# Decoder layer: the down projection's buffers laid out anew, and the work behind the last unit of the up projection put in another order

## The chip, the cores and the metric

The kernel runs on one core of one Trainium2 chip. The metric is the device time of one execution in microseconds (us). A profiled execution is the source of all views shown here; times inside it count from the start of its span.

## The reference

One decoder layer on 1024 tokens with 1024 channels, float32. Three branches (an mLSTM, a differential attention, a cross-attention into 256 memory tokens) are merged by gates and projected; then comes the MLP, which is the part this change touches:

```python
D_MODEL = 1024
SEQ = 1024
D_FF = 4 * D_MODEL
...
        x = x + merged @ w_out[l]

        h2 = rms_norm(x, norm_mlp_g[l])
        x = x + jnp.square(jax.nn.relu(h2 @ w_up[l])) @ w_down[l]
```

## The kernel before, in words

Float32 products are made from three passes of TensorE: every operand is split into a rounded part and the rest (`split`, lines 106 to 117: ScalarE casts, VectorE subtracts), and `mm3` (line 88) issues three matmuls, first*first, first*rest, rest*first. Nearly all matmuls of the kernel stand therefore under line 93.

The MLP is computed with seven products in place of eight for each 2x2 block of tiles (Winograd's form of Strassen's scheme). `PROD` lists the seven pairs: which of seven sums of weights meets which of seven sums of activations. A *step* is one such block: 7 products x 3 = 21 matmuls of 128x512.

Up projection, `wino`: 16 *units*. Each has four steps (one for each pair of input blocks `kp`), and its seven products gather in seven of PSUM's eight banks `p0` to `p6`; the next unit takes the banks shifted by one. After a unit VectorE combines the seven banks into four tiles (`c11`, `u2`, `u3`, `c21`), and `use_up` multiplies them by the normalisation `rb`, ScalarE takes relu and square into `rq`, and `wino_t` makes four sums `xts` of the squares (lines 1242 to 1245: t0 = b0-b1, t2 = b2-b0 on GpSimd always, t1 = b2-t0, t3 = b3-t1). The three plain tiles (`r_d<-rq`, issued by ScalarE) and the four sums (`r_d<-xts`, issued by SyncE) are stored to the DRAM buffer `r_d`, one entry for each unit: 7 planes of 128x512. Unit u is operand q = u of the down projection.

Down projection, `down`: 16 passes of four steps, `passes = [(p % 4, range(p, 4 + p))]`. Pass p works for output group p % 4 with operands q = p to p + 3. An operand is fetched back from `r_d` in two or three parts into `xd` tiles (`xdma`: three planes and four, or 3 + 2 + 2), and each part is split in place (`xsplit`: ScalarE cast, VectorE subtract). Operand 0 lies in pools x00 (planes 0 to 2), x01 (3, 4) and x02 (5, 6); operands 1, 2, 3 in x1, x2, x3; later ones take these places over in turn. This text calls the two parts of operands 1 to 3 "1a" (three planes) and "1b" (four planes) and so on; 4a, 4b, 4c are the three parts of operand 4.

Weights, `wino_steps`: `raw()` loads 256 KB of raw weights (`wraw`, SyncE) and has GpSimd make four sums of 128x128 (lines 1260 to 1263); `wsp(n)` splits the seven sums into a weight pair `wo` (ScalarE cast, VectorE subtract, 128x896 each) and issues the next `raw()`. `wrp` and `wop` are rings of places for raw weights and pairs, `lead` says how many steps ahead of its use a pair is made. `side(n)`, called behind step n, makes the next pair, fetches the operand whose place has come free, and splits parts of the one that is needed two or three steps later.

The sums over passes lie in SBUF accumulators `acc`. Behind the first pass of each group four of them are loaded with the residual (`acc<-x_d`, 256 KB each, SyncE), VectorE subtracts one from another, and then adds the banks to them; the next pass may overwrite a bank only when that has been done.

What sets the order: TensorE and all VectorE work that goes through `self.V` (class `InOrder`) stand in the order of the program text while `self.pinned` is set. Everything on `nc.scalar`, `nc.gpsimd`, `nc.sync` and plain `nc.vector` (so also `self.split`, in contrast to `self.split2`) is placed in its engine's queue by the scheduler of the build. Each engine then runs its queue strictly in order. SyncE's queue holds nearly all loads and stores: a store that waits for its data holds back all loads behind it. Pools are laid into SBUF one behind the other, so which place of `down` lies on which place of `wino` decides when the first loads of `down` may start.

Of the kernel before, what the change touches and what calls it, by code (L numbers as in the profile page):

```python
# [73 lines left out]
class Layer:  # L74
# [1340 lines left out]
    def tail(self):  # L1415
        tc, nc, a = self.tc, self.nc, self.a
        V, G = nc.vector, nc.gpsimd
# [9 lines left out]
        with ExitStack() as c0:  # L1427
# [4 lines left out]
            rb = one.tile([P, D], F32, name="rb2")  # L1432
# [63 lines left out]
            with ExitStack() as c1:  # L1496
                E = lambda *x, **k: c1.enter_context(tc.tile_pool(*x, **k))
                one_ = lambda n: E(name=n, bufs=1)
# [17 lines left out]
                def use_up(u, cs):  # L1516

                    b = self.xrp.tile([P, 4, 512], F32, tag="xr", name=self.name("rq"))
                    V_, M = (nc.vector, G) if u == 15 else (self.V, self.V)
                    for i in (1, 3, 2, 0):  # L1520
                        hf = i % 2
                        M.tensor_mul(cs[i], cs[i], rb[:, hf * 512 : (hf + 1) * 512])
                        self.A.activation(cs[i], cs[i], AF.Relu)
                        self.A.activation(b[:, i], cs[i], AF.Square)
                    self.A.dma_start(self.rd[u, :, 0:3], b[:, 1:4])
                    yield
                    t = self.wino_t(b, V_)
                    nc.sync.dma_start(self.rd[u, :, 3:7], t)
                    yield

# [34 lines left out]
    def down(self):  # L1565
# [4 lines left out]
        with ExitStack() as c1:  # L1570
            one_ = lambda n: c1.enter_context(tc.tile_pool(name=n, bufs=1))

            def accum(pool, n, pad):
                accs.extend(pool.tile([P, 512], F32, name=f"acc{len(accs) + i}") for i in range(n))
                if pad:
                    pool.tile([P, pad], F32, name=self.name("pad"))
# [8 lines left out]
            wr = [one_("dwr0"), one_("dwr1")]  # L1585
            a2 = one_("acc2")
            accum(a2, 4, 0)
            wr.append(one_("dwr2"))
            a3 = one_("acc3")
            accum(a3, 8, 768)  # L1590
            x1, x2 = one_("dx1"), one_("dx2")
            x02, wr = one_("dx02"), Ring(wr)
            wo = Ring([one_(f"dwo{i}") for i in range(3)])
            x00 = one_("dx00")
            accs = accs[2:] + accs[:2]
            xp = (((x00, 0, 3), (x01, 3, 2), (x02, 5, 2)), *(((x, 0, 3), (x, 3, 4)) for x in (x1, x2, x3)))
            acc = [accs[7 * g : 7 * g + 7] for g in range(4)]
# [5 lines left out]
            passes = [(p % 4, tuple(range(p, 4 + p))) for p in range(16)]  # L1603
            last = len(passes) - 1
            steps = [(g, q) for g, qs in passes for q in qs]
            raw, wsp, W = self.wino_steps([a["wdown"][g][:, kp(q)] for g, q in steps], wr, wo, 2)
            X, use1, use9 = {}, {}, {}
            for n, (g, q) in enumerate(steps):
                use1.setdefault(q, n)
# [2 lines left out]
            def xdma(q):  # L1612

                X[q] = []
                for pool, i, n in xp[q % 4]:
                    t = pool.tile([P, n, 2, 512], F32R, tag=f"x{i}", name=self.name("xd"))
                    nc.sync.dma_start(f32(t[:, :, 1]), self.rd[kp(q), :, i : i + n])
                    X[q].append(t)
# [22 lines left out]
                        xsplit(q, (1, 2))  # L1641

            xdma(0)
            raw()
            raw()
            xsplit(0, split=self.split)
            wsp(0, self.split, False)
            xdma(1)
            xsplit(1, split=self.split)
            wsp(0)  # L1650
            xdma(2)
            xsplit(2, (0,))
            wsp(0)
            xsplit(2, (1, 2))
            xdma(3)
            n = -1
            seen = set()
            for p, (g, qs) in enumerate(passes):
# [7 lines left out]
                for run in (qs[0:1], qs[1:2], qs[2:4]) if p == last else [(q,) for q in qs]:  # L1666
                    for j, (l, x) in enumerate(self.PROD):
                        for i, q in enumerate(run):
                            w = W[n + 1 + i]
                            self.mm3(ps[j], (w[:, l, 0], w[:, l, 1]), operand(q, x), q == qs[0], q == qs[-1])  # L1670
                    n += len(run)
                    if q != qs[-1]:
                        side(n)
                if new:

# [230 lines left out]
```

## Time and profile before

| what | value |
|---|---|
| median of three runs | 2195.51 us (2194.28 to 2201.09) |
| the profiled execution's own time | 2196.3 us |
| its span (first to last instruction) | 2194.5 us |
| TensorE (PE) matmul busy | 2150.9 us, 98% of the span |
| VectorE (DVE) busy | 1418.6 us, 65% |
| ScalarE (ACT) busy | 1002.7 us, 46% |
| GpSimd (POOL) busy | 565.5 us, 26% |
| mean granted TensorE clock | 0.996 |
| up projection, matmuls out of `xo` | 1344, 307.0 us busy |
| down projection, matmuls out of `xd` | 1344, 310.5 us busy, the first at 1871.98 us |

The profile's rows read "start us, us, engine, line, operation, out<-in, how many in a row, and in brackets the idle time before with what ended it". Buffer numbers are left out there: `wo` is any weight pair, `xd` any part of an operand, `p` any PSUM bank. SPq is SyncE's queue. The table says that TensorE sets the time; what can be won or lost by a change at the joint of the two projections is idle time of TensorE there, and the matmuls that it then runs at a lower clock.

### The profile page before, as it was taken

Reading aid. Unit: us, or ns where it says so; the run is one execution under the profiler, and the core shown is the slowest. Engines: PE = TensorE matmul, PEld = TensorE weight load, DVE = VectorE, ACT = ScalarE, POOL = GpSimd, SP = SyncE. Lnnn points to the kernel's source line nnn. Section 1 sums busy time; section 2 is a strip of 40 time slices with the busy share of each in tenths; the row PEclk is TensorE's granted clock in tenths of the full one; section 3 lists DMA queues with packets and bytes.
Section 4 is the critical chain, followed back from the end, with each engine's and each line's share of the span. In section 5 each row is a group of like instructions: output and inputs, shape, how many; then the busy total and the mean of one; then the engine's idle time right before and its main releaser. Section 6 shows DMA issues by size and latency. Waiting matters only on the chain.

```text
span 2194.5 us, 30706 instructions
## 1 busy us (share of the span) xinstructions
PE 2150.9 (98%) x11049; PEld 1852.4 (84%) x11049; DVE 1418.6 (65%) x2674; ACT 1002.7 (46%) x1998; POOL 565.5 (26%) x736
## 2 busy tenths in 40 slices
PE   7999999999999999999999999999999999899999
PEld 5877888898899999999888788888888788688887
DVE  6643565575548778777655433554688987767779
ACT  6543354454346666666554221223435444543332
POOL 2100000000111111111121002202756665655552
PEclk9999999999999999999999999999999999999999
DMA  6123122121443433333343643435434544844444
GB/s 246 36 73 116 59 92 68 45 81 49 161 115 92 96 97 91 84 84 83 109 148 133 207 143 127 146 111 191 154 121 173 194 155 148 328 163 158 142 142 168
DMA packets 137358, 281.46 MB, mean 128 GB/s; under 512 B 13137, under 2 KB 29814, under 8 KB 135158
## 3 DMA queue, kind: packets, MB, share of 16 engines
q1 hardware_dynamic: 130870, 259.58, 37.5%
q10 hardware_dynamic: 6336, 19.93, 2.3%
q8 instruction: 87, 1.43, 0.3%
q14 instruction: 65, 0.53, 0.1%
HBM read 182.95 MB, written 71.34 MB: 116 GB/s over the span
## 4 chain that ended last, share of the span: by engine, by line
PE 87%; DVE 5%; DMA 3%; ACT 2%; issue 1%; POOL 1%; SPq 0%; DVEq 0%; ACTq 0%; POOLq 0%
PE mm L93 51%; PE p L93 23%; PE sc L93 6%; PE po L93 3%; PE tp L96 3%; DVE acc L69 1%; DVE u L69 1%; PE pr L96 1%; DMA kraw<-y 1%; DVE wo L69 0%; DMA xd<-r_d 0%; DVE c L69 0%; PE tp L93 0%; DVE w L114 0%; DMA mx<-in_mem 0%
## 5 line engine op out<-in xcount | busy, mean ns | idle before, releaser
L93 PE MATMUL mm<-w,hT 128*128 128x384 f32 (+3 forms) x2496 | 470.6, 330 | 4.1 <-ACT w L113 3.5
L93 PE MATMUL mm<-hT,w 128*128 128x512 f32 x1680 | 413.2, 397 | 0.0
L93 PEld LDWEIGHTS mm<-w,hT 128*128 128x128 f32 x2496 | 387.7, 189 | 15.9 <-ACT w L113 4.3
L93 PEld LDWEIGHTS mm<-hT,w 128*128 128x128 f32 x1680 | 309.6, 189 | 65.1
L93 PE MATMUL p<-xd,wo 128*128 128x512 f32 x1344 | 310.5, 393 | 7.4 <-DVE xd L69 1.6
L93 PE MATMUL p<-xo,wo 128*128 128x512 f32 x1344 | 307.0, 390 | 1.2 <-DVE u L69 1.2
L93 PEld LDWEIGHTS p<-xd,wo 128*128 128x128 f32 x1344 | 253.7, 189 | 64.1 <-DVE xd L69 2.6
L93 PEld LDWEIGHTS p<-xo,wo 128*128 128x128 f32 x1344 | 251.6, 188 | 55.2 <-DVE u L69 2.8
L93 PE MATMUL mm<-kt,w 128*128 128x512 f32 x1152 | 264.1, 391 | 4.7 <-ACT kt L113 3.6
L93 PEld LDWEIGHTS mm<-kt,w 128*128 128x128 f32 x1152 | 216.9, 189 | 51.8 <-ACT kt L113 4.7
L113 ACT CAST w<-raw 128x256 fp32r<-128x256 f32 (+3 forms) x272 | 142.1, 545 | 166.6 <-PE mm L93 120.2
L106 ACT CAST wo<-wraw 128x896 fp32r<-128x896 f32 x124 | 116.8, 944 | 213.7 <-PE p L93 98.4
L114 DVE TENSOR_TENSOR w<-raw,w 128x256 fp32r<-128x256 f32 (+3 forms) x272 | 161.5, 614 | 79.9 <-ACT w L113 79.0
L69 DVE TENSOR_TENSOR wo<-wraw,wo 128x896 fp32r<-128x896 f32 x124 | 143.6, 1172 | 59.1 <-ACT wo L106 59.1
L1260 POOL TENSOR_TENSOR wraw<-wraw 128x128 f32<-128x128 f32 x128 | 93.7, 732 | 246.2 <-DMA wraw<-in_wdown 109.5
L1008 ACT ACTIVATE dpe<-sc,dst,drr 128x256 f32<-128x256 f32 (+7 forms) x128 | 106.6, 833 | 97.5 <-DVE dst L1004 95.2
L129 POOL TENSOR_SCALAR hss<-hss 128x4 f32<-128x4 f32 x8 | 3.3, 408 | 414.9 <-ACT mscr L754 273.0
L1000 DVE CUSTOM_DVE_ANT_0 sc<-sc,tmask 128x256 f32<-128x256 f32 (+7 forms) x128 | 97.0, 758 | 13.3 <-PE sc L93 12.7
L93 PE MATMUL sc<-dk,dq 128*128 128x512 f32 (+3 forms) x384 | 92.2, 348 | 0.0
L106 ACT CAST xd<-xd 128x1536 fp32r<-128x1536 f32 (+2 forms) x38 | 58.3, 1535 | 68.6 <-DMA xd<-r_d 68.6
L1263 POOL TENSOR_TENSOR wraw<-wraw 128x128 f32<-128x128 f32 x128 | 86.6, 676 | 10.0
L1262 POOL TENSOR_TENSOR wraw<-wraw 128x128 f32<-128x128 f32 x128 | 88.9, 694 | 0.0
(313 smaller groups left out, 3083.9 us busy)
## 6 DMA issues: line engine op xcount, KB each, us to landing
dk<-dsg SPq DMA_DIRECT2D x64, 256.0 KB, 4.5
wraw<-in_wup SPq DMA_DIRECT2D x64, 256.0 KB, 2.9
r_d<-xts SPq DMA_DIRECT2D x16, 1024.0 KB, 4.1
wraw<-in_wdown SPq DMA_DIRECT2D x64, 256.0 KB, 3.0
xd<-r_d SPq DMA_DIRECT2D x19, 768.0 KB, 7.3
xd<-r_d SPq DMA_DIRECT2D x14, 1024.0 KB, 6.4
raw<-in_wd SPq DMA_DIRECT2D x32, 384.0 KB, 3.3
gl<-gates SPq DMA_DIRECT2D x48, 256.0 KB, 2.7
```

Of the source, the lines that this page charges most:

```text
L69: return self.tc.keep_in_program_order(f(*a, **k))
L93: self.pin(self.nc.tensor.matmul(out, l, r, start=start, stop=stop))
L96: self.pin(self.nc.tensor.transpose(out, x, self.ident))
L106: self.A.copy(hi, src)
L113: nc.scalar.copy(hi, src)
L114: nc.vector.tensor_sub(lo, src, f32(hi))
L129: g.tensor_scalar(r, ss, 1.0 / width, EPS, op0=ALU.mult, op1=ALU.add)
L1000: V.tensor_tensor_reduce(out=sc[:, 0:n], in0=sc[:, 0:n], in1=self.tmask[:, D - n : D], scale=1.0, scalar=-3.0e38, op0=ALU.add, op1=ALU.max ...
L1008: nc.scalar.activation(pe[c][:, 0:n], sc[:, 0:n], AF.Exp, bias=t8[:, 2 + c : 3 + c], scale=rr[:, i, c : c + 1], accum_out=t8[:, 4 + c : 5 ...
L1260: G.tensor_add(r[:, 4], r[:, 0], r[:, 3])
L1262: G.tensor_sub(r[:, 6], r[:, 1], r[:, 0])
L1263: G.tensor_sub(r[:, 7], r[:, 2], r[:, 5])
```

## The change

It touches three things.

1. Places. `down` now has four places for raw weights and four for pairs (three each before), pairs are made three steps ahead (`lead` 3, before 2), and the last part of operand 0, x02, has a place at the top of SBUF. By the addresses of the build, x02 lay on two raw places of the up projection before, and lies on no place of it now; the four raw places and four pair places are now just those of the up projection.
2. The start of `down`: four raw loads first, then operands 1, 2 and 3 in one go; x02 of operand 0 is split beside x00 and x01; three pairs are made with `self.split` ahead of the first pass, and operand 2 is left to `side`.
3. Behind the last unit (u = 15): the four multiplications by `rb` go from GpSimd to VectorE, in the pinned order; three of the four sums `xts` go from VectorE to GpSimd, which then makes all four; and what `side(0)` issues on VectorE stands behind the last of the four multiplications (`tc.issue_after`).

```diff
                     b = self.xrp.tile([P, 4, 512], F32, tag="xr", name=self.name("rq"))
-                    V_, M = (nc.vector, G) if u == 15 else (self.V, self.V)
                     for i in (1, 3, 2, 0):
                         hf = i % 2
-                        M.tensor_mul(cs[i], cs[i], rb[:, hf * 512 : (hf + 1) * 512])
+                        self.after = self.V.tensor_mul(cs[i], cs[i], rb[:, hf * 512 : (hf + 1) * 512])
...
-                    t = self.wino_t(b, V_)
+                    t = self.wino_t(b, G if u == 15 else self.V)
...
-            wr.append(one_("dwr2"))
+            wo = [one_("dwo0")]
             a3 = one_("acc3")
-            accum(a3, 8, 768)
+            accum(a3, 8, 0)
             x1, x2 = one_("dx1"), one_("dx2")
-            x02, wr = one_("dx02"), Ring(wr)
-            wo = Ring([one_(f"dwo{i}") for i in range(3)])
-            x00 = one_("dx00")
+            wr = Ring(wr + [one_("dwr2"), one_("dwr3")])
+            wo = Ring(wo + [one_(f"dwo{i}") for i in (1, 2, 3)])
+            x00, x02 = one_("dx00"), one_("dx02")
...
-            raw, wsp, W = self.wino_steps([a["wdown"][g][:, kp(q)] for g, q in steps], wr, wo, 2)
+            raw, wsp, W = self.wino_steps([a["wdown"][g][:, kp(q)] for g, q in steps], wr, wo, 3)
...
             xdma(0)
-            raw()
-            raw()
+            for _ in range(4):
+                raw()
+            xdma(1)
+            xdma(2)
+            xdma(3)
+            xsplit(2)
             xsplit(0, split=self.split)
-            wsp(0, self.split, False)
-            xdma(1)
+            wsp(0, self.split)
             xsplit(1, split=self.split)
-            wsp(0)
-            xdma(2)
-            xsplit(2, (0,))
-            wsp(0)
-            xsplit(2, (1, 2))
-            xdma(3)
+            wsp(0, self.split)
+            wsp(0, self.split)
...
-                    if q != qs[-1]:
+                    if n == 0:
+                        with tc.issue_after(self.after.ins):
+                            side(n)
+                    elif q != qs[-1]:
                         side(n)
```

How the built programs differ at three places. First VectorE's queue about 150 us before the end of the up projection, where the combining of a unit meets the splits of operand 0; with `xd` the parts x01 (2 planes) and, in the changed program, x02. Before:

```order
L69 TENSOR_TENSOR u2_2678_16878<-u2_2678_16878,p2_2666_16756 128x512
L114 TENSOR_TENSOR xd_2849_18252<-xd_2849_18252 128x2x512
L69 TENSOR_TENSOR u3_2680_16880<-u2_2678_16878,p3_2667_16757 128x512
L69 TENSOR_TENSOR c21_2681_16881<-u3_2680_16880,p4_2668_16758 128x512
L69 TENSOR_TENSOR u3_2680_16880<-u3_2680_16880,p5_2669_16759 128x512
```

The same place of the changed program:

```order
L69 TENSOR_TENSOR u2_2678_16878<-u2_2678_16878,p2_2666_16756 128x512
L114 TENSOR_TENSOR xd_2848_18257<-xd_2848_18257 128x2x512
L69 TENSOR_TENSOR u3_2680_16880<-u2_2678_16878,p3_2667_16757 128x512
L114 TENSOR_TENSOR xd_2849_18259<-xd_2849_18259 128x2x512
L69 TENSOR_TENSOR c21_2681_16881<-u3_2680_16880,p4_2668_16758 128x512
```

A second split now stands between two combining steps of that unit; it stood at the joint before.

Second, GpSimd's queue behind the last unit: `wraw` are raw weights of `down`, `xts_2845` the four sums of the last unit out of its squares `rq_2844`. Before, from the last multiplication on:

```order
L1522 TENSOR_TENSOR u2_2840_18120<-u2_2840_18120,rb2_13027 128x512
L1243 TENSOR_TENSOR xts_2845_18146<-rq_2844_18132 128x512
L1260 TENSOR_TENSOR wraw_2871_18343<-wraw_2871_18343 128x128
L1262 TENSOR_TENSOR wraw_2871_18343<-wraw_2871_18343 128x128
L1261 TENSOR_TENSOR wraw_2871_18343<-wraw_2871_18343 128x128
```

The changed program, from the last sum of the fifth raw load (numbered from 0 in the prediction: raw 4) on; four sums of raw 4 stand ahead of this piece:

```order
L1263 TENSOR_TENSOR wraw_2861_18310<-wraw_2861_18310 128x128
L1260 TENSOR_TENSOR wraw_2863_18323<-wraw_2863_18323 128x128
L1262 TENSOR_TENSOR wraw_2863_18323<-wraw_2863_18323 128x128
L1261 TENSOR_TENSOR wraw_2863_18323<-wraw_2863_18323 128x128
L1263 TENSOR_TENSOR wraw_2863_18323<-wraw_2863_18323 128x128
L1260 TENSOR_TENSOR wraw_2865_18332<-wraw_2865_18332 128x128
L1242 TENSOR_TENSOR xts_2845_18146<-rq_2844_18132 128x512
L1243 TENSOR_TENSOR xts_2845_18146<-rq_2844_18132 128x512
L1244 TENSOR_TENSOR xts_2845_18146<-rq_2844_18132,xts_2845_18146 128x512
L1261 TENSOR_TENSOR wraw_2865_18332<-wraw_2865_18332 128x128
L1245 TENSOR_TENSOR xts_2845_18146<-rq_2844_18132,xts_2845_18146 128x512
```

Before, one sum of `xts` stood here, next behind the multiplication; now all four do, behind nine sums of raw weights and with a tenth among them.

Third, SyncE's queue from the last part of an operand ahead of the last store on: `xd_2874` before, and `xd_2877` now, is part 4c. Before:

```order
L1617 DMA xd_2873_18351<-r_d 128x2x512
L1617 DMA xd_2874_18353<-r_d 128x2x512
L1528 DMA r_d<-xts_2845_18146 128x2048
L1274 DMA wraw_2876_18381<-in_wdown 128x512
L1274 DMA wraw_2878_18413<-in_wdown 128x512
L1677 DMA acc4_18188<-x1_d 128x512
L1677 DMA acc14_18193<-x1_d 128x512
L1677 DMA acc10_18191<-x1_d 128x512
L1677 DMA acc12_18192<-x1_d 128x512
```

The changed program:

```order
L1616 DMA xd_2876_18377<-r_d 128x2x512
L1527 DMA r_d<-xts_2845_18146 128x2048
L1274 DMA wraw_2874_18369<-in_wdown 128x512
L1616 DMA xd_2877_18379<-r_d 128x2x512
L1274 DMA wraw_2879_18407<-in_wdown 128x512
L1274 DMA wraw_2881_18439<-in_wdown 128x512
L1678 DMA acc4_18188<-x1_d 128x512
L1678 DMA acc14_18193<-x1_d 128x512
L1678 DMA acc10_18191<-x1_d 128x512
L1678 DMA acc12_18192<-x1_d 128x512
```

In both the four accumulators stand behind the last store of `xts`; one more raw load and part 4c now stand between them.

## The prediction

> **What bounds the kernel now.** I read the totals first, then the timeline of TensorE across the joint of the two projections, then the chain of waits there, then what the engines in the chain did. The totals:
>
> ```profile
> PE 2150.9 (98%) x11049; PEld 1852.4 (84%) x11049; DVE 1418.6 (65%) x2674; ACT 1002.7 (46%) x1998; POOL 565.5 (26%) x736
> ```
>
> TensorE is the bound, and no matmul is added or removed. So the change acts through TensorE's idle time and its clock. Its timeline over the joint (each row: start, length, count, idle before with its releaser):
>
> ```profile
> 1871.98 1.52 PE L93 MATMUL p<-xd,wo 128*128 128x512 f32 x6
> 1874.88 0.96 PE L93 MATMUL p<-xd,wo 128*128 128x512 f32 x3 [1.38 <-DVE c L69]
> 1876.60 2.51 PE L93 MATMUL p<-xd,wo 128*128 128x512 f32 x9 [0.76 <-POOL wraw L1261]
> 1879.53 10.55 PE L93 MATMUL p<-xd,wo 128*128 128x512 f32 x45 [0.42 <-DVE u L69]
> 1891.64 0.50 PE L93 MATMUL p<-xd,wo 128*128 128x512 f32 x1 [1.56 <-ACT wo L106]
> 1893.77 0.51 PE L93 MATMUL p<-xd,wo 128*128 128x512 f32 x1 [1.64 <-DVE xd L69]
> 1895.89 24.33 PE L93 MATMUL p<-xd,wo 128*128 128x512 f32 x90 [1.61 <-DVE wo L69]
> ```
>
> Matmul 91 of the down projection, the first that overwrites a bank of pass 0 behind the residual, is decisive. The chain of waits, and the store ahead of it on SyncE's queue:
>
> ```profile
> 1893.64 0.94 DVE xts L1245
> 1895.87 0.55 SPq L1274
> ...
> 1898.62 4.99 DMA acc<-x_d
> 1903.70 0.06 DVE acc L69
> ...
> 1904.47 0.68 DVE acc L69
> 1905.19 4.83 PE p L93 x20
> 1894.64 0.33 SPq L1528 DMA_DIRECT2D r_d<-xts  x1
> ```
>
> The last subtraction of the last unit ends at T = 1893.64 + 0.94 = 1894.58; the store goes at once, two raw loads and four accumulators are queued behind it, and matmul 91 starts at 1905.19, 10.61 us after T. The clock and the rates there, by windows (busy time and count of PE, PEld, DVE, ACT, POOL, granted clock, DMA share, GB/s), with a full-speed window for comparison:
>
> ```profile
> 1870.00:1875.00 5.00, 3.62 (x17) 2.69 (x16) 4.74 (x4) 3.23 (x3) 1.85 (x3) 1.00 1.02 406
> 1895.00:1900.00 5.00, 4.11 (x9) 2.86 (x10) 4.30 (x3) 3.81 (x5) 1.15 (x1) 0.56 0.91 290
> 1900.00:1905.00 5.00, 5.00 (x18) 3.74 (x16) 1.30 (x2) 3.73 (x5) 4.11 (x10) 0.75 1.05 397
> 2100.00:2150.00 50.00, 50.00 (x222) 41.40 (x222) 43.63 (x48) 18.93 (x18) 25.66 (x39) 1.00 0.57 184
> ```
>
> A matmul at full clock takes 50/222 = 0.225 us. After the idle of 1890 to 1896 the clock was 0.56 and 0.75 in two windows: (0.44 + 0.25) x 5 = 3.45 us of work lost. Before, that loss lay ahead of matmul 91, which waited for the accumulators anyway; so it cost little.
>
> **Part 1: the split of x02, moved into a combining chain of the up projection.**
>
> ```profile
> 1721.43 1.76 PE L93 MATMUL p<-xo,wo 128*128 128x512 f32 x6 [0.77 <-DVE u L69]
> 1723.61 36.56 PE L93 MATMUL p<-xo,wo 128*128 128x512 f32 x160 [0.43 <-DVE u L69]
> 1719.56 1.22 DVE L114 TENSOR_TENSOR xd<-xd 128x1024 fp32r<-128x1024 f32 x1
> ```
>
> TensorE already waits here for VectorE's combining (0.77 + 0.43), with one split of two planes in the chain. A second, of the same shape, goes in two steps later. Nothing covers it, so it costs its full 1.22 us at most, and nothing if its data or the banks come in another order: bounds 0 to 1.2. I take +1.2, as the waits show no slack. The matching ScalarE cast runs beside other work. What this delays, it delays for all that follows; the times below are in the frame of before.
>
> **Part 2: loads at the joint.** x02 (512 KB) no longer loads there, and a raw load of 256 KB goes ahead of the rush. What stands behind both, part 3b, lands 768 KB earlier in the stream, which at 406 GB/s is 1.9 us. Its issue, and the row of its landing (KB, us to landing):
>
> ```profile
> 1870.13 1.63 SPq L1617 DMA_DIRECT2D xd<-r_d  x1
> xd<-r_d SPq DMA_DIRECT2D x1, 1024.0 KB, 13.9
> ```
>
> 1870.1 + 13.9 = 1884.0 becomes 1882.1; raw 4 stands behind it (256 KB, 0.65 us): 1882.8. Raw 5 and raw 6 follow.
>
> **Part 3: the last unit.** VectorE takes the four multiplications, ahead of the splits of operands 2 and 3. The rows that price them, and ScalarE's squares of the unit before:
>
> ```profile
> 1856.05 1.28 DVE L69 TENSOR_TENSOR c<-c,rb 128x512 f32<-128x512 f32 x2
> 1874.15 0.68 DVE L69 TENSOR_TENSOR c<-u,p 128x512 f32<-128x512 f32 x1
> 1878.19 1.29 DVE L69 TENSOR_TENSOR u<-u,p 128x512 f32<-128x512 f32 x2
> 1882.24 0.67 DVE L69 TENSOR_TENSOR u<-u,p 128x512 f32<-128x512 f32 x1
> 1856.76 1.24 ACT L1523 ACTIVATE c<-c 128x512 f32<-128x512 f32 x2 [2.63 <-DVE c L69]
> 1859.99 1.14 ACT L1524 ACTIVATE rq<-u 128x512 f32<-128x512 f32 x2
> ```
>
> Part 1b, whose split precedes c11, lands 256 KB (0.65 us) earlier, so c11 goes at 1873.5 instead of 1874.15. The combining to 1879.48 then ends at 1878.8, and the last addition (0.67), no longer behind a split, at 1879.5. Two pairs of multiplications (1.28 each): 1882.0. Squares: 1856.05 to 1859.99 + 1.14 is 5.1 us from first multiplication to last square, so they are ready at 1879.5 + 5.1 = 1884.6; before, they took until about 1889.4. By itself that is a gain of 5 us.
>
> But the four subtractions `xts` now all stand on GpSimd, behind nine sums of raw 4, 5 and 6 and with a tenth among them. Prices: the sums of 1870 to 1900 (min/median/max ns), an unhindered one, a 128x512 operation, and the one subtraction that GpSimd did before:
>
> ```profile
> L1260 POOL TENSOR_TENSOR wraw<-wraw x3: 901/1395/1988, 1873.1 to 1891.2; 128x128 f32<-128x128 f32 x3
> L1262 POOL TENSOR_TENSOR wraw<-wraw x3: 449/466/1967, 1874.5 to 1892.1; 128x128 f32<-128x128 f32 x3
> L1261 POOL TENSOR_TENSOR wraw<-wraw x3: 897/1300/1317, 1874.9 to 1894.0; 128x128 f32<-128x128 f32 x3
> L1263 POOL TENSOR_TENSOR wraw<-wraw x3: 454/1185/2390, 1876.3 to 1895.0; 128x128 f32<-128x128 f32 x3
> 1900.38 0.45 POOL L1260 TENSOR_TENSOR wraw<-wraw 128x128 f32<-128x128 f32 x1 [4.23 <-DMA wraw<-in_wdown]
> 1886.77 1.28 POOL L1522 TENSOR_TENSOR u<-u,rb 128x512 f32<-128x512 f32 x1
> 1889.46 1.77 POOL L1243 TENSOR_TENSOR xts<-rq 128x512 f32<-128x512 f32 x1 [1.41 <-ACT rq L1524]
> ```
>
> The same 128x128 sum takes 0.45 us while VectorE is idle and up to 2.39 us while VectorE subtracts. In the changed program VectorE has splits and pairs (2a, 2b, a pair, 3a, a pair, 3b) to run in that stretch, so I use the medians: four sums 1.395 + 0.466 + 1.300 + 1.185 = 4.35; nine are 2 x 4.35 + 1.40 = 10.1; then 4 x 1.77 + 1.30 = 8.4. T = 1882.8 + 10.1 + 8.4 = 1901.3, 6.7 us later than before. The bounds: nothing hindered, 1882.8 + 9 x 0.45 + 4 x 1.28 + 0.45 = 1892.4; every sum at its maximum, 7.66 for four, 1882.8 + 17.3 + 7.1 + 1.3 = 1908.5. I stand by the medians, as they were taken with VectorE as busy as it will be.
>
> By the Trainium skill (*SBUF — State Buffer*, "Who interferes with whom") VectorE's and GpSimd's shared port pair is an exclusive lock, held for a two-input operation of either; the 2.39 beside the 0.45 agrees with it. By that rule T lies at the medians or above, without it at 1892.4.
>
> From T to matmul 91: 10.6 before. Part 4c (512 KB) and one raw load (256 KB) now stand in between, 768 KB or 1.9 us: 12.5. Matmul 91 starts at 1901.3 + 12.5 = 1913.8, 8.6 us later. Nothing hides that. What TensorE does ahead of it (an earlier pair removes some of the three waits of 1.6 us) is done at about 1900 and only lengthens the idle time.
>
> **Part 4: the clock.** The idle time of some 13 us now ends at matmul 91, so the slow matmuls come behind it and are paid in full. Samples: 3.45 above, and this one:
>
> ```profile
> 1215.77 16.41 PE L93 MATMUL mm<-kt,w 128*128 128x512 f32 x63 [2.95 <-ACT kt L113]
> ```
>
> 63 x 0.225 = 14.2, so 2.2 lost. I take the mean, +2.8.
>
> The Trainium skill (*TensorE: Matmul & The Clock Gate*, "What's actually happening") has half the clock until one window of 3.4 us has been busy, an estimated 1.7 us of loss, which would give a sum lower by 1.1 us; the rows above show 2.2 and 3.45, more than that.
>
> **Part 5: the end.** Pairs are made a step earlier, and the last pair no longer comes late:
>
> ```profile
> 2169.62 20.31 PE L93 MATMUL p<-xd,wo 128*128 128x512 f32 x88
> ```
>
> 88 x 0.225 = 19.8, so at most 0.5 us is to be had there; I take -0.5. Steps between have no waits in the timeline and gain nothing from `lead` 3.
>
> **The sum.** 2196.3 (the profiled execution) + 1.2 + 8.6 + 2.8 - 0.5 = 2208.4. That execution is 0.8 us above the median of 2195.5, so I forecast 2207.6. A measurement of this kernel can tell about 0.3%, 6.6 us, from no change. By the same sum the break-even lies at T = 1905.2 - 12.5 - 1.2 - 2.8 + 0.5 = 1889.2, and slower by 6.6 us at T = 1895.8.
>
> **The rivals.** (a) *GpSimd is not held up.* If VectorE is idle when the sums run, because its splits are done or wait for data, T is 1892.4, matmul 91 at 1904.9 (-0.3), idle time before it some 4 us, clock loss 2.2: 2196.3 + 1.2 - 0.3 + 2.2 - 0.5 = 2198.9, 2198 on the median's scale, no change. For it: raw 4 to 6 have no pair to wait for. Against: in 1870 to 1900 nearly every sum was held up. This is the one on the other side, and it decides from T = 1895.8 down.
>
> (b) *The standstill goes.* Squares 5 us earlier and pairs a step earlier are the gain that the edit offers. If the accumulators landed in time, matmul 91 would start between 1892.25 (no wait at all: 1871.98 + 90 x 0.225) and about 1898 (one wait for a split left): 7 to 13 us gained, less 0.7 for the rest, 2183 to 2189, mean 2186. It needs T at 1885.5 or earlier, but the squares are ready at 1884.6 and four subtractions take 4 x 1.28 = 5.1. Only if these found GpSimd free and the loads were quicker than in the rows could it be.
>
> (c) *Worse.* T at its upper bound 1908.5 puts matmul 91 at 1921.0: 7.2 us more, 2215.
>
> **How the numbers follow.** Forecast 0.65, with a range of its own of 2202 to 2212 (T from 1895.8 to 1905.5); (a) 0.17; (b) 0.10; (c) 0.08. (b) and half of (c) may stay outside: 2194 to 2214. Faster by over 0.3%: most of (b), 0.09. Slower: the forecast and (c), 0.73. The rest, 0.18, is no change.
>
> **What would show it.** In the changed profile: at 1720 a wait about 1.2 us longer before a matmul of the up projection; the nine sums ahead of the first L1242 on GpSimd mostly at 0.9 to 2.4 us, not 0.45; the store `r_d<-xts` at about 1902; a wait of TensorE of 10 us or more ended by `acc`, and a clock under 1 behind it. A store ahead of 1896 would make the forecast wrong, as would the accumulators landing without it, or sums of 0.45.

## The result, and the profile after

The changed kernel takes 2206.2 us (median of 6 runs, 2202.2 to 2208.1), the kernel before 2196.2 us beside it: ratio 1.0042, 95% interval 1.003 to 1.0054. Timed again at the end, with other runs of before, it took 2207.8 against 2195.3: 1.0047 (1.0035 to 1.006). So it is slower by 10 to 12.5 us. The forecast was 2207.6, with a range of 2194 to 2214.

TensorE over the joint after the change (the columns are those of the timeline of before):

```profile
1877.58 7.31 PE L93 MATMUL p<-xd,wo 128*128 128x512 f32 x31 [0.42 <-DVE u L69]
1885.19 5.09 PE L93 MATMUL p<-xd,wo 128*128 128x512 f32 x21 [0.30 <-DVE xd L69]
1892.12 4.83 PE L93 MATMUL p<-xd,wo 128*128 128x512 f32 x20 [1.84 <-DVE xd L69]
1912.36 12.88 PE L93 MATMUL p<-xd,wo 128*128 128x512 f32 x44 [15.41 <-DVE acc L69]
```

(Ahead of these rows stand waits of 1.11 and 0.62 us.) Of the three waits of 1.6 us that stood there before, 0.30 + 1.84 are left; TensorE then reaches matmul 91 at 1896.95 and stands still for 15.41 us, until 1912.36. The chain of waits of the same execution, in the stretch that ends there:

```profile
1899.57 0.33 SPq L1527
...
1904.75 6.18 DMA acc<-x_d
```

The store of the last unit goes out at 1899.57; the last of the four accumulators is issued by 1904.75 and lands 6.18 us later, at 1910.93, and VectorE's subtraction and addition stand between that and matmul 91. What made the store late is GpSimd's own timeline: nine sums of raw 4, 5 and 6, then the subtractions L1242 to L1245 with a tenth sum among them:

```profile
1880.53 0.52 POOL L1260 TENSOR_TENSOR wraw<-wraw 128x128 f32<-128x128 f32 x1 [12.80 <-DMA wraw<-in_wdown]
1881.01 1.98 POOL L1262 TENSOR_TENSOR wraw<-wraw 128x128 f32<-128x128 f32 x1
1882.95 2.50 POOL L1261 TENSOR_TENSOR wraw<-wraw 128x128 f32<-128x128 f32 x1
1885.53 1.19 POOL L1263 TENSOR_TENSOR wraw<-wraw 128x128 f32<-128x128 f32 x1
1886.68 1.97 POOL L1260 TENSOR_TENSOR wraw<-wraw 128x128 f32<-128x128 f32 x1
1888.62 1.30 POOL L1262 TENSOR_TENSOR wraw<-wraw 128x128 f32<-128x128 f32 x1
1889.88 2.50 POOL L1261 TENSOR_TENSOR wraw<-wraw 128x128 f32<-128x128 f32 x1
1892.46 0.46 POOL L1263 TENSOR_TENSOR wraw<-wraw 128x128 f32<-128x128 f32 x1
1892.88 0.46 POOL L1260 TENSOR_TENSOR wraw<-wraw 128x128 f32<-128x128 f32 x1
1893.30 1.30 POOL L1242 TENSOR_TENSOR xts<-rq 128x512 f32<-128x512 f32 x1
1894.54 2.15 POOL L1243 TENSOR_TENSOR xts<-rq 128x512 f32<-128x512 f32 x1
1896.65 1.26 POOL L1244 TENSOR_TENSOR xts<-rq,xts 128x512 f32<-128x512 f32 x1
1897.88 0.45 POOL L1261 TENSOR_TENSOR wraw<-wraw 128x128 f32<-128x128 f32 x1
1898.29 1.25 POOL L1245 TENSOR_TENSOR xts<-rq,xts 128x512 f32<-128x512 f32 x1
```

Six of the nine sums take 1.2 to 2.5 us; the two behind them, when VectorE has run dry, take 0.46. The last subtraction ends at T = 1898.29 + 1.25 = 1899.54. The clock behind the standstill (windows: busy and count of PE, PEld, DVE, ACT, POOL, granted clock, DMA share, GB/s):

```profile
1910.00:1915.00 5.00, 2.64 (x6) 2.15 (x7) 3.98 (x6) 0.00 (x0) 0.80 (x2) 0.50 1.03 397
1915.00:1920.00 5.00, 5.00 (x17) 3.93 (x16) 3.07 (x4) 0.94 (x1) 1.98 (x5) 0.70 0.56 127
```

From 1912.36 to 1915 the clock is 0.50, and in the next 5 us 0.70 on average: 2.64 x 0.50 + 5 x 0.30 = 2.8 us of work lost, all of it behind matmul 91. And the place in the up projection where the split of x02 went:

```profile
1717.64 0.97 PE L93 MATMUL p<-xo,wo 128*128 128x512 f32 x3 [0.76 <-DVE u L69]
1719.37 1.15 PE L93 MATMUL p<-xo,wo 128*128 128x512 f32 x3 [0.77 <-DVE c L69]
1720.77 9.46 PE L93 MATMUL p<-xo,wo 128*128 128x512 f32 x35 [0.24 <-DVE u L69]
```

The waits were 0.77 + 0.43 and are 0.76 + 0.77 + 0.24.

**Where the time went, matmul by matmul.** Both programs have 11049 matmuls in the same order, and the same work on every engine up to the loading and splitting of x02. So the start of the n-th matmul can be compared from trace to trace. The table gives these differences to the profile of before, in us, for all kernels of this study (the numbers are those of the experiments below): at matmul 9000 (behind nothing but unchanged work), what the step at 1720 adds (matmul 9000 to 9200), what the joint adds (9200 to 11000; the last 49 give back 0.2 us in all but number 7), and the change of the medians beside it. The last two columns are in the *frame of before*: each profile's times are shifted by as much as its matmul 9600, just ahead of the joint, was early or late. They give T, the end of the last unit's last subtraction, and how much later matmul 91 starts; before, T was 1894.6.

| kernel | at matmul 9000 | step at 1720 | joint | step + joint | median against before | T | matmul 91 |
|---|---|---|---|---|---|---|---|
| changed kernel | -3.80 | +2.18 | +11.40 | +13.6 | +10.0 | 1901.2 | +8.8 |
| changed kernel, second profile | -5.87 | +0.95 | +10.97 | +11.9 | +12.5 | 1900.8 | +8.4 |
| 1 subtractions ahead of the sums | -3.03 | +0.96 | +3.91 | +4.9 | +5.0 | 1893.7 | +3.9 |
| 2 no subtraction in two splits | -2.96 | +0.99 | +2.72 | +3.7 | +1.4 (one run) | 1894.1 | +1.1 |
| 3 accumulators ahead of the store | -0.99 | +0.96 | +0.47 | +1.4 | +1.0 | 1901.2 | -2.9 |
| 4 both 1 and 3 | -2.23 | +0.95 | +1.66 | +2.6 | +1.0 | 1893.2 | +1.8 |
| 5 split of x02 later | -0.98 | +0.01 | +10.89 | +10.9 | +10.5 | 1900.4 | +8.0 |
| 6 places and start alone | +2.22 | +2.14 | -1.06 | +1.1 | +1.2 | 1890.0 | -0.9 |
| 7 last unit alone | -0.82 | -0.05 | +6.37 | +6.3 | +8.6 | 1899.6 | +5.0 |
| 8 best: 4 and two more edits | +2.35 | -0.90 | -0.72 | -1.6 | -3.4 | 1894.7 | -3.4 |
| 9 store on GpSimd | -2.62 | +0.96 | +2.79 | +3.8 | +2.2 | 1901.3 | -4.2 |
| 10 store on GpSimd, two more edits | -1.38 | -0.93 | +1.70 | +0.8 | +0.4 | 1901.7 | -5.6 |
| 11 three subtractions on VectorE | +0.32 | +0.95 | +7.54 | +8.5 | +6.4 | 1898.3 | +5.5 |

The first column is the spread of one execution from the next on identical work: 8 us, larger than most of what is to be explained. That is why the joint is read from the traces here, and the medians only confirm it; the two agree within 2.5 us for all but the first row. Of the 11.4 us that the joint adds in the first profile, 6.6 come from the later T, 2.2 from the longer way from T to matmul 91 (12.8 us in place of 10.6) and 2.6 from the clock behind it. Where the accumulators stand behind the store (the changed kernel, numbers 1, 2, 5, 7 and 11), matmul 91 comes 10.6 to 15.4 us after T; in numbers 9 and 10, where they do not, it starts ahead of T.

### The profile page after: what moved, and what is told of

It reads as the page before. It is cut to its first block, busy times and chain, and to the rows that moved or that the text cites. A ratio compares the mean times of both kernels' runs of the same rounds, so it can differ in the third digit from the quotient of the medians.

```text
span 2204.0 us, 30703 instructions
## 1 busy us (share of the span) xinstructions
PE 2149.0 (98%) x11049; PEld 1850.2 (84%) x11049; DVE 1417.9 (64%) x2675; ACT 1002.9 (46%) x1998; POOL 565.2 (26%) x735
## 4 chain that ended last, share of the span: by engine, by line
PE 88%; DMA 4%; DVE 3%; ACT 2%; POOL 1%; issue 1%; SPq 1%; DVEq 0%; ACTq 0%; POOLq 0%
PE mm L93 51%; PE p L93 24%; PE sc L93 6%; PE po L93 3%; PE tp L96 3%; PE pr L96 1%; DMA wraw<-in_wdown 1%; DMA kraw<-y 0%; PE tp L93 0%; DVE acc L69 0%; DMA hx<-hc_d 0%; DVE w L114 0%; DMA mx<-in_mem 0%; DVE u L69 0%; DMA xk<-in_x 0%
## 5 line engine op out<-in xcount | busy, mean ns | idle before, releaser
L93 PE MATMUL p<-xd,wo 128*128 128x512 f32 x1344 | 309.4, 392 | 19.7 <-DVE acc L69 15.4
L1000 DVE CUSTOM_DVE_ANT_0 sc<-sc,tmask 128x256 f32<-128x256 f32 (+7 forms) x128 | 97.1, 759 | 12.6 <-PE sc L93 12.2
```

Source lines behind the costliest of these rows:

```text
L93: self.pin(self.nc.tensor.matmul(out, l, r, start=start, stop=stop))
L1000: V.tensor_tensor_reduce(out=sc[:, 0:n], in0=sc[:, 0:n], in1=self.tmask[:, D - n : D], scale=1.0, scalar=-3.0e38, op0=ALU.add, op1=ALU.max ...
```

## The experiments

My theory ahead of them: the last unit's subtractions are late (T) because on GpSimd they stand behind nine sums, each held up by VectorE; TensorE waits because the accumulators stand behind their store on SyncE's queue. Rivals: the step in the up projection, the places, or the sheer amount of work of the two engines.

**1. Subtractions ahead of the nine sums.** `self.xlast` is the last subtraction; the sums of raw 4, 5 and 6 are issued behind it.

```diff
-            wsp(0, self.split)
-            xsplit(1, split=self.split)
-            wsp(0, self.split)
-            wsp(0, self.split)
+            for i in range(3):
+                wsp(0, self.split, False)
+                if i == 0:
+                    xsplit(1, split=self.split)
+                with tc.issue_after(self.xlast.ins):
+                    raw()
```

> Only the order on GpSimd is changed on purpose: the four subtractions of the last unit stand ahead of the sums of raw 4, 5 and 6 (the build then also puts one raw load between the second and the third accumulator load). In the changed kernel's profile the last subtraction ends at T = 1899.5 and matmul 91 starts at 1912.4. Theory (T is set by the place behind nine sums): the squares are ready at 1883.3, four subtractions of 1.3 to 2.1 us follow, T = 1888.5 to 1891.5. Raw 4 pays: its sums end near 1895, its pair near 1897.5, so matmul 85 comes 5 us later than now (1890.8 to 1892.1 unhindered); and one raw load that waits for a pair stands ahead of two accumulators, so matmul 91 is at 1905 to 1908 and the time 2199 to 2202. Rival (the chain does not run through the store; the nine sums are not what is late): T moves but matmul 91 stays at 1912 and the time at 2206.

Measured: 2200.38 us, ratio 1.0026 (1.0017 to 1.0034). GpSimd's subtractions, SyncE's queue and TensorE:

```profile
1883.07 2.36 POOL L1242 TENSOR_TENSOR xts<-rq 128x512 f32<-128x512 f32 x1 [15.63 <-DMA xd<-r_d]
1885.38 2.13 POOL L1243 TENSOR_TENSOR xts<-rq 128x512 f32<-128x512 f32 x1
1887.48 2.80 POOL L1244 TENSOR_TENSOR xts<-rq,xts 128x512 f32<-128x512 f32 x1
1890.35 1.27 POOL L1245 TENSOR_TENSOR xts<-rq,xts 128x512 f32<-128x512 f32 x1
```

```profile
1899.62 0.33 SPq L1274 DMA_DIRECT2D wraw<-in_wdown  x1
1900.28 5.49 SPq L1680 DMA_DIRECT2D acc<-x_d  x10
```

```profile
1898.38 6.62 PE L93 MATMUL p<-xd,wo 128*128 128x512 f32 x20 [7.54 <-DVE xd L69]
1907.04 18.20 PE L93 MATMUL p<-xd,wo 128*128 128x512 f32 x79 [2.03 <-DVE acc L69]
```

T = 1891.6, matmul 91 at 1907.04: as the theory had it. T is 7.5 us earlier than in the changed kernel (in the frame of before), and half of the loss is gone by the medians, two thirds of the joint by the traces. Two things are to be seen. The four subtractions, now met by VectorE's splits, take 1.3 to 2.8 us each, 8.5 in all, against 1.25 to 2.15 above. And the raw load between the accumulators waits for a pair until 1899.62, so that two accumulators go out more than 8 us behind T.

**2. VectorE without the splits of operands 2 and 3.**

```diff
             def xsplit(q, parts=(0, 1, 2), split=self.split2):
+                if q in (2, 3):
+                    split = lambda hi, lo, src: self.A.copy(hi, src)
```

> VectorE's subtraction is left out in the splits of operands 2 and 3 (the rest of these operands is then the unsplit value), so that VectorE has only two pairs to make while GpSimd forms the sums of raw 4, 5 and 6. GpSimd's order is as in the changed kernel. Theory (GpSimd and VectorE shut each other out): most of the nine sums take 0.45 us in place of the 0.5 to 2.5 us there; they end near 1885 to 1888, T = 1890 to 1892 in place of 1899.5. Rival (the sums are slow for the transfers that run at that time, or by themselves): sums of 1 to 2.5 us as before, T within 2 us of 1899.5.

This kernel leaves VectorE's part of these splits out and serves for its times alone. Measured in one execution: GpSimd's first sum, the one that was held up, and the last subtraction.

```profile
1881.04 0.46 POOL L1260 TENSOR_TENSOR wraw<-wraw 128x128 f32<-128x128 f32 x1 [13.94 <-DVE wo L69]
...
1884.24 1.19 POOL L1263 TENSOR_TENSOR wraw<-wraw 128x128 f32<-128x128 f32 x1
...
1890.82 1.30 POOL L1245 TENSOR_TENSOR xts<-rq,xts 128x512 f32<-128x512 f32 x1
```

Eight of the nine sums take 0.46 to 0.47 us; the one of 1.19 falls on the only subtraction that VectorE has in that time, of a pair, at 1883.89 to 1885.10. T = 1890.82 + 1.30 = 1892.1 in place of 1899.5, 7 us earlier in the frame of before. The transfers are not what lengthens the sums: in the changed kernel the DMA engines were busy for 0.13 of the time from 1885 to 1890 and not at all from 1890 to 1895, while four sums took 1.2 to 2.5 us; here they were busy for 0.56 from 1880 to 1885, and the sums took 0.46. So it is VectorE's subtractions. The Trainium skill (*SBUF — State Buffer*, "Who interferes with whom") has it as an exclusive lock that the one who starts later waits for; 0.46 against 2.50 us for the same sum agrees. TensorE still waits for the accumulators, from 1893.5 to 1904.34; matmul 91 comes 12.2 us after T:

```profile
1904.34 20.95 PE L93 MATMUL p<-xd,wo 128*128 128x512 f32 x84 [10.82 <-DVE acc L69]
```

**3 and 4. The accumulators ahead of the store; and this with 1.** The four loads of the first group are issued behind those of raw 4 to 6 (`resid(0)`), and no longer behind the first pass.

```diff
             wsp(0, self.split)
             wsp(0, self.split)
+            resid(0)
             n = -1
...
-                    for j, f, hf in ((1, 0, 1), (6, 0, 0), (4, 1, 1), (5, 1, 0)):
-                        nc.sync.dma_start(A[j], half(self.x1d, 2 * g + f, hf))
+                    if g:
+                        resid(g)
```

> The four accumulator loads of the first group are issued behind the loads of raw 4, 5 and 6, ahead of the store of the last unit; all else as in the changed kernel (the build then puts the loads of operand 4 behind the store). Theory (matmul 91 waits for the last subtraction only through SyncE's queue): T stays near 1899.5, the accumulators land before 1890, the wait of 15.4 us ahead of matmul 91 goes, and it starts at 1897 to 1898. The low clock goes with it (2.8 us). New waits of 1 to 4 us are likely near matmul 148, since operand 4 now loads behind the store. Time 2188 to 2194, faster than before the change. Rival (the joint is bound by VectorE, GpSimd or the stream of loads anyway): another wait of 8 us or more follows within the next 60 matmuls, time 2200 or more.

> Both edits: accumulator loads ahead of the store, and the four subtractions ahead of the nine sums on GpSimd. Theory: matmul 91 no longer hangs on T, so an earlier T (1888.5 to 1891.5) is of no use to it; the sums of raw 4 are late instead and matmul 85 waits until near 1897.5. Operand 4 loads 9 us earlier, which takes away waits at matmul 148. Time within 3 us of the kernel with the accumulator loads alone: 2188 to 2195. Rival (T itself is what counts): at least 5 us faster than the kernel with the accumulator loads alone.

Measured: 2196.45 us, 1.0003 (0.9994 to 1.0012), for the loads alone, 2196.37, 1.0009 (1.0 to 1.0018), for both. The mechanism was right, the times were 2.5 and 1.4 us above my ranges. TensorE with the loads alone:

```profile
1892.35 0.49 PE L93 MATMUL p<-xd,wo 128*128 128x512 f32 x1 [1.42 <-ACT xd L106]
1894.68 8.39 PE L93 MATMUL p<-xd,wo 128*128 128x512 f32 x23 [1.83 <-DVE xd L69]
1903.53 14.16 PE L93 MATMUL p<-xd,wo 128*128 128x512 f32 x61 [0.46 <-ACT acc L1689]
1918.78 0.96 PE L93 MATMUL p<-xd,wo 128*128 128x512 f32 x3 [1.09 <-DVE xd L69]
```

T is 1901.2, as late as in the changed kernel, and the wait of 15 us is gone: the late store costs mainly through what is queued behind it. Matmul 91 starts at 1902.2, not at 1897 to 1898 as I expected. Waits of 1.42, 1.83, 0.46 and 1.09 us stay, and a clock of one half behind them, and use up the gain over before. With both edits a wait of 7.53 us stands ahead of matmul 71, and VectorE's row before it shows why:

```profile
1898.63 61.64 PE L93 MATMUL p<-xd,wo 128*128 128x512 f32 x260 [7.53 <-DVE xd L69]
```

```profile
1894.93 1.19 DVE L69 TENSOR_TENSOR wo<-wraw,wo 128x896 fp32r<-128x896 f32 x1 [5.55 <-ACT wo L106]
```

Operand 3's second split stands behind the pair of raw 4, whose sums are now behind the subtractions: VectorE waited 5.55 us for their cast, and that split came at 1896.04. As expected, an earlier T brought nothing once matmul 91 did not hang on it.

**5. The split of x02 later.** It is issued behind the last addition of that unit.

```diff
-            xsplit(0, split=self.split)
+            xsplit(0, (0, 1), split=self.split)
+            with tc.issue_after(self.comb[6].ins):
+                xsplit(0, (2,), split=self.split)
```

> The changed kernel with VectorE's split of x02 behind the last addition of that unit, where VectorE sits idle for 1.6 us, and nothing else changed. Theory (the move costs TensorE one more wait in the combining chain, as measured by matmul times: 1.0 us in three of four profiles, 2.2 in the one where a low clock came with it): the waits at 1720 go back from 0.77 + 0.77 + 0.43 to 0.77 + 0.43, time 1 us less than the changed kernel, 2204 to 2205.5, still slower than before. The joint stays as it is: T near 1899.5, a wait of 13 to 16 us ahead of matmul 91. Rival (the move is what made the kernel slower): 2200 or less.

Measured: 2205.92 us, 1.0047 (1.0034 to 1.006).

```profile
1720.46 1.75 PE L93 MATMUL p<-xo,wo 128*128 128x512 f32 x6 [0.76 <-DVE u L69]
1722.64 7.55 PE L93 MATMUL p<-xo,wo 128*128 128x512 f32 x32 [0.43 <-DVE u L69]
```

The step falls from 0.95 to 0.01 us in the trace and the joint stays at +10.9 (the wait ahead of matmul 91 is 12.48 us, just under the expected 13 to 16). In the medians (2205.9, 0.4 above my range, against 2206.2 and 2207.8) so small a gain can't be told. The rival is out: the move is not what made the kernel slower.

**6 and 7. The two halves of the change, each alone.** Number 6 is the changed kernel with the last unit's work as before and without the fixed order; number 7 the kernel before with the new work behind the last unit.

> The places and the start of the down projection as in the changed kernel, the work behind the last unit as before the change (multiplications on GpSimd, three subtractions on VectorE in the scheduler's order, no fixed order). The build then puts VectorE's subtractions of the last unit ahead of the splits of operand 2 and the one on GpSimd behind seven sums. Theory: VectorE waits for the squares (near 1884), so operand 2's split comes near 1890 and matmul 43 waits about 9 us there; T is 1889 to 1892, and matmul 91 then comes near 1903 to 1906: 2197 to 2203, slower by less than the whole change. Rival (the places alone are a gain, and the last unit's order is what lost it): 2192 or less.

> The places and the start of the down projection as before the change, with the new work behind the last unit (multiplications on VectorE, all four subtractions on GpSimd, the fixed order). GpSimd then has the four sums of one raw load, which lands near 1884.7, ahead of the subtractions, in place of nine of three loads. Theory: sums until 1889, four subtractions of 1.3 to 2.1 us, T = 1894.5 to 1897.5, within 3 us of before's 1894.6, matmul 91 at 1905 to 1908, time 2194 to 2199. Rival (taking the subtractions to GpSimd is by itself what costs the time): T near 1899.5 and 2203 or more.

Measured: places and start alone 2196.67 us, 1.0002 (0.9993 to 1.0011), no loss that can be told (operand 2's late split cost one wait of 3.28 us, not the 9 that I expected, and T came at 1890.0 in the frame of before); the last unit alone 2204.06, 1.0035 (1.0022 to 1.0048). So nearly all of the loss belongs to the last unit's work. For number 7 my theory missed, and the rival's numbers came true. GpSimd there, behind four sums, not nine:

```profile
1889.24 2.01 POOL L1242 TENSOR_TENSOR xts<-rq 128x512 f32<-128x512 f32 x1 [0.77 <-ACT rq L1523]
...
1893.31 3.34 POOL L1244 TENSOR_TENSOR xts<-rq,xts 128x512 f32<-128x512 f32 x1
1896.73 2.02 POOL L1245 TENSOR_TENSOR xts<-rq,xts 128x512 f32<-128x512 f32 x1
```

T = 1898.75, in the frame of before 1899.6, only about 1.5 us earlier than behind nine sums, and matmul 91 follows 10.6 us later, as it did before. The sums did not delay it: the first subtraction waited 0.77 us for the squares, which in this order of VectorE's work came at 1889.2. The subtractions themselves then took 2.0 to 3.3 us, 9.5 in all, while VectorE was still splitting. I had counted 5 to 8 for them. So the place behind the sums is one way to a late T, not the only one.

**8. The best version.** Number 4, and at step 1 operand 3's second split ahead of the pair (`wsp` behind `xsplit` in `side(1)`), and the splits of x01 and x02 behind the unit's last addition.

> From the two edits together (accumulators ahead of the store, subtractions ahead of the nine sums), two more: at step 1 operand 3's second split stands ahead of the pair of raw 4 on ScalarE and VectorE, and the splits of x01 and x02 stand behind the unit's last addition. Theory: what held matmul 71 for 7.5 us in the kernel with both edits was that pair, which waits for the late sums, ahead of operand 3's split; now the split ends near 1892, matmul 71 waits 1 to 2 us, matmul 85 waits 1 to 3 us for the pair, and one of the three waits at 1720 stays (0.4). Time 2187 to 2191, faster than before the change by 0.2 to 0.4%. Rival (the joint is held by the total of VectorE's and GpSimd's work, whatever the order): another wait of 5 us or more, time 2194 to 2198.

Measured: 2192.02 us, 0.9986 (0.9977 to 0.9995): faster than the kernel before by 0.14%, and, by the differences to it, 13 to 16 us faster than the changed kernel. It missed its range (2187 to 2191) by 1 us.

```profile
1891.79 1.66 PE L93 MATMUL p<-xd,wo 128*128 128x512 f32 x6 [1.17 <-DVE xd L69]
1895.09 3.45 PE L93 MATMUL p<-xd,wo 128*128 128x512 f32 x14 [1.64 <-DVE xd L69]
1899.29 0.74 PE L93 MATMUL p<-xd,wo 128*128 128x512 f32 x2 [0.75 <-ACT wo L106]
1900.51 1.63 PE L93 MATMUL p<-xd,wo 128*128 128x512 f32 x4 [0.49 <-DVE wo L69]
1903.24 56.93 PE L93 MATMUL p<-xd,wo 128*128 128x512 f32 x238 [1.09 <-DVE acc L69]
```

The waits of 1.17 and 7.53 of number 4 have become five of 0.5 to 1.6, 5.1 in all: the rival was half right, the work of VectorE and GpSimd fills much of the joint in this order too.

**9 and 10. The last store on GpSimd's own queue,** behind its last subtraction; number 10 with the two further edits of number 8.

```diff
-                    nc.sync.dma_start(self.rd[u, :, 3:7], t)
+                    (G if u == 15 else nc.sync).dma_start(self.rd[u, :, 3:7], t)
```

> The changed kernel with one edit: the store of the last unit's four sums is issued by GpSimd, behind its own last subtraction, in place of SyncE. Theory (the subtractions cost time only because everything behind their store on SyncE's queue waits for them): T stays at 1899 to 1901, but the accumulators go out when their queue reaches them, behind the raw load that waits for the pair of raw 4 (near 1891), and land near 1895 to 1896; matmul 91 follows matmul 90 within 1 us, at 1897 to 1899; operand 4 is loaded before T. Time 2190 to 2195. Rival (the late subtractions hold TensorE in another way, or VectorE and GpSimd are simply full): another wait of 8 us or more within the next 60 matmuls, 2200 or more.

> The store on GpSimd's queue as in the run above, and two more edits of the best kernel so far: operand 3's second split ahead of the pair of raw 4, and the splits of x01 and x02 behind the unit's last addition. The sums of raw 4 stay ahead of the subtractions. Theory: waits ahead of matmuls 64 to 71 of 1 to 3 us in all, matmul 85 and 91 without a wait over 1 us, one wait of 0.4 at 1720: 2187 to 2191, at least as fast as the best kernel so far (2192.0). Rival (a store on that queue delays the sums of raw 6 and 7 behind it, and so matmuls 127 and 148): 2193 or more.

Measured: 2197.51 us, 1.0007 (0.9998 to 1.0016), and 2195.75, 1.0003 (0.9994 to 1.0012); both above my ranges. One line of the program takes 8 us off the joint, which shows once more that the way from T to TensorE is SyncE's queue. What I had overlooked is another engine's queue, ScalarE's and TensorE's rows of number 9:

```profile
1901.24 0.94 ACT L106 CAST wo<-wraw 128x896 fp32r<-128x896 f32 x1 [9.22 <-POOL wraw L1263]
...
1903.46 1.06 ACT L1684 COPY acc<-p 128x512 f32<-128x512 f32 x2
```

```profile
1904.09 56.26 PE L93 MATMUL p<-xd,wo 128*128 128x512 f32 x234 [3.92 <-ACT acc L1684]
```

Two of the copies that free banks of the first pass (L1684) stand behind the cast of raw 6's pair, that waits for its sums until 1901.2, and these stand behind the subtractions on GpSimd (and behind the issue of the store, 0.75 us). The late subtractions hold TensorE by a second way, for 3.92 us. In number 10 it is the same: a wait of 3.83 us for such a copy, and one of 2.47 for the accumulators ahead of matmul 91, where I expected none over 1 us. So its rival's time of 2193 or more came true; its reason, the store's place on that queue, accounts for the 0.75 us alone.

**11. Three of the four subtractions back on VectorE.**

```diff
-                    t = self.wino_t(b, G if u == 15 else self.V)
+                    t = self.wino_t(b, nc.vector if u == 15 else self.V)
```

> The changed kernel with three of the last unit's four subtractions back on VectorE (the fourth stays on GpSimd behind the nine sums, as it stood on GpSimd before); multiplications on VectorE, places and store as changed. The build puts them ahead of the splits of operand 2. Theory (each engine's work there adds to the other's, and the queue position sets T): T is set by the one subtraction on GpSimd, 1893 to 1896; matmul 43 waits until 1888 for operand 2, matmul 91 comes at 1904 to 1908; time 2198 to 2203, 3 to 8 us less than the changed kernel. Rival (it does not matter which engine subtracts): T at 1899 or later, 2205 or more.

Measured: 2201.71 us, 1.0025 (1.0013 to 1.0036): the time as expected, T and matmul 91 not, so that the time is in part luck. The one subtraction that GpSimd keeps:

```profile
1897.48 2.13 POOL L1243 TENSOR_TENSOR xts<-rq 128x512 f32<-128x512 f32 x1
```

It ends at 1899.6 (1898.3 in the frame of before), though three fewer stand beside it: the nine sums ahead of it, from 1884.21 on, took 13.3 us with VectorE's additional work, against 12.8 and 10.5. Matmul 91 starts at 1911.99, not at 1904 to 1908, behind waits of 4.65 us for operand 2, 4.83 for a copy on ScalarE and 1.91 for the accumulators.

**12. The changed kernel once more.**

> The changed kernel once more, unaltered, for a second profile beside the others of this series. Theory: the half-clock window near 1720 and the early start of the up projection (3.8 us ahead of the profile of before, by the same instructions) were chance: here the step at 1720 costs 1.0 us, the joint 10.5 to 11.5, and the median is 2204 to 2208. Rival (they belong to the change): the step costs 2.2 us again, and the up projection starts 3 to 4 us ahead of before's again.

Measured: 2207.78 us, 1.0047 (1.0035 to 1.006). The step is 0.95, the joint 10.97. In the first profile and in number 6 the step was 2.2 and 2.1; the waits there sum to nearly the same (1.77 and 1.76 against 1.96), and a clock of one half for 3.4 us fell on them. Its profiled execution started even earlier than the first one, 5.87 us, and was the fastest of the five (2202.05). Number 5, which differs from it in one split, started 0.98 us early, and numbers 6, 8 and 11, with the same work up to there, started late, so I take the early start for chance too, though two of two profiles have it.

## Why the prediction was right, point by point

In the frame of before (the first profile's times + 1.62, by which its matmul 9600 was early; the second's + 4.92):

| step | predicted | first profile | second profile |
|---|---|---|---|
| step at 1720 | +1.2 | +2.18 | +0.95 |
| first sum of raw 4 | 1882.8 | 1882.2 | 1881.9 |
| nine sums | 10.1 | 12.8 | 10.5 |
| the rest to T | 8.4 | 6.2 | 8.3 |
| T | 1901.3 | 1901.2 | 1900.8 |
| T to matmul 91 | 12.5 | 12.8 | 12.9 |
| matmul 91 | 1913.8 | 1914.0 | 1913.6 |
| clock behind it | +2.8 | +2.6 | +2.6 |
| end | -0.5 | -0.2 | -0.2 |

(The clock is the joint less the delay of matmul 91: 11.40 - 8.8 and 10.97 - 8.4.)

The sum of 12.1 stands against 10.0 and 12.5 by the medians. Four points:

- **T was right, its explanation in part.** I wrote that the subtractions are late as they stand behind nine sums. Number 1 shows that the order matters to TensorE (T 7.5 us earlier, half of the loss gone), but in 7 T is only about 1.5 us earlier with the sums done in time, by late squares and by subtractions that take 9.5 us beside VectorE's splits, and in 11 under 3 us earlier with a single subtraction. What these have in common is that GpSimd and VectorE work here nearly as one engine. By the unhindered lengths in these traces, GpSimd's work up to T is 10 x 0.45 + 4 x 1.27 = 9.6 us, and VectorE's from 1880.64 on 1.76 + 2.29 + 1.76 + 2.29 for the splits and 3 x 1.08 for the pairs = 11.3. The sum, 20.9, is near the 19.0 us from the first sum to T; side by side it would be 11.3. In the first profile the sums had the contention and the subtractions little of it, so that my two terms were off by 2.7 and 2.2 us in opposite directions and cancelled: that T came within 0.1 us there is luck. In the second they came out one by one.
- **The clock** was the right size for the reason given: the slow matmuls lie behind the wait and are paid. The Trainium skill (*TensorE: Matmul & The Clock Gate*, "What's actually happening") counts one window of 3.4 us, an estimated 1.7 us lost; here 2.8 us were lost by the windows above, as much as 5.6 us at one half (5.5 in the second profile): more than one such window, as it would be if the restart fell inside one, which no run here tests. One of my two samples was a little too large: in the 3.45 I counted whole windows, but TensorE came back at 1895.89 and had half the clock until 1902.45, which is 3.3 lost and leaves the term at 2.8.
- **The step of x02** was 0.95 where I had 1.22. VectorE's two additions around the second split started 0.79 us apart before (1720.69 and 1721.48) and 1.74 now (1716.90 and 1718.64): the second addition reads what the first one wrote and started 0.79 us behind it, while the split starts 0.60 us behind it and holds the addition for 1.14 more, so that it adds 0.95 and not its whole length.
- **The rivals.** That GpSimd is not held up is refuted by its rows (six of nine sums at 1.2 us or more, five in the second profile), and number 2 is what it would have looked like. That the standstill goes took the four edits of number 8, and gave 3.4 us, not 7 to 13.

The expectations of 3, 4, 8, 9 and 10 were all too fast by 1 to 5 us. The same step failed each time: I took away the longest wait and counted its whole length as gain, while waits of 0.5 to 4 us (7.5 in number 4) of the two filled engines came next, and a half clock with them.

## What to carry to other kernels

Before handing work from VectorE to GpSimd, add up what both have to do in that stretch as if it were one engine, when it is two-input arithmetic out of SBUF as here: 20.9 us of work took 19.0, so the hand-over saved little, and it put the result behind the other queue. Ask then who waits for the late result by the queue alone: a store on the queue of the loads held TensorE for 15 us for data that none of those loads needed. And once the longest wait is removed, price the next ones on every in-order queue, ScalarE's copies among them, before counting the gain.

## What I had not expected of the hardware

A 1 MB store issued by GpSimd held that engine for only 0.75 us (1899.97 to 1900.72 in number 9), less than two of its small sums. And one execution differs from the next by up to 8 us at the same matmul, on identical work. A good part of it lies in half-clock windows of 3.4 us (up to 1.7 us of work lost in each) that follow waits of 1 to 3 us between 110 and 1222 us: none in the first profile of the changed kernel, two in that of before, four in numbers 6, 8 and 11. So a difference of two single profiles says nothing until the matmuls are aligned.
